# A three-matmul float32 trunk: the token forms of the output products change sides in SBUF, and the weights get a fourth place

## The chip, the cores and the metric

The kernel runs on one core of one Trainium2 chip, as one launch. The metric is the device time of that launch in microseconds (us), from the first to the last instruction and what lies around them; less is better. The core has five engines that run side by side, each through a list of instructions of its own, in order: PE (TensorE, matrix products; PEld in the profile is its weight load), DVE (VectorE), ACT (ScalarE), POOL (GpSimd) and SP (which here only issues transfers). SBUF is the on-chip memory: 128 partitions, and in each of them a run of bytes; "low" and "high" mean the byte address in a partition. PSUM is where PE puts its sums. A wait between engines is a semaphore.

## The reference, cut to what matters

A decoder trunk over 1024 tokens of width 1024, in float32: a mixing layer with a gated linear recurrence (HGRN2) and a stick-breaking attention, a channel MLP, a gMLP layer, a second channel MLP, a last norm.

```python
for layer in range(2):
    h = rms_norm(x, mix_norm[layer])
    if layer == 0:
        proj = h @ ab_w_in[0]                    # 1024 x 3584
        ...                                      # recurrence and attention
        mix = concat([oa, ob]) @ ab_w_out[0]     # 1024 x 1024
    else:
        gated = chunked_gmlp(h @ gm_w_in[0], ln_g, ln_b, gm_ws, gm_bs)   # 1024 x 6144
        mix = gated @ gm_w_out[0]                # 3072 x 1024
    x = x + mix
    h = rms_norm(x, mlp_norm[layer])
    x = x + square(relu(h @ mlp_w1[layer])) @ mlp_w2[layer]    # 1024 x 4096, 4096 x 1024
return rms_norm(x, final_norm)
```

## The kernel before, in words

**Every product is three matmuls.** A float32 operand is split into `hi`, its value rounded to the matmul's float32r (an ACT copy, L190 or L738), and `lo`, the rest (a DVE subtract, L191 or L739). `mm3` (L181 to L183) then adds hi by hi, hi by lo and lo by hi into one PSUM tile. A matmul has a stationary operand of 128 x 128, loaded by PEld, and a moving one of 128 x 512; the profile writes `acc<-f1h,whi` for a moving `f1h` over a stationary `whi`.

**The big matrix products go by seven instead of eight.** From about 640 us on each weight matrix is cut in blocks of 2 x 2, and a block's product is made of seven products P1 to P7 of sums of sub-blocks (*forms*), on the weights' side and on the tokens' side. There are three pairs of stages: *inward* (`inward`: `w1`, `gm_in`, `w1` of the second MLP) with 8, 6 and 8 blocks, and *outward* (`outward`: `w2`, `gm_out`, `w2`) with 4, 3 and 4. Before the second pair `gmlp` makes the half of `gm_in` that is normed; there the tokens are the stationary operand.

- In *inward* the seven token forms are made once for a stage (`form0` and `half1_forms`, L836 to L866) and stay; the weights are loaded (`raw`), added to forms on DVE (L888 to L896) and split into `whi` and `wlo`. One product is 24 matmuls, in the order P1, P2, P6, P7, P5, P4, P3. Results go through `x` tiles and are stored to `f_d` as the next stage's token forms by POOL (L939).
- In *outward* a product is 48 matmuls: both its token forms come from `f_d` into the tiles `fb` and are split into `f1h` and `f1l`, which then move over the weights, one half of them in `raw`, `whi`, `wlo`, the other in `fr`, `fh`, `fl`. Results are added to the `x` tiles (L1065).

**Tags.** All these tiles are 4096 bytes in a partition and belong to a tag with a number of places. A tile's split may only start when the place that it gets has been left by its last reader. Before the change: `raw` 6 places, `whi` and `wlo` 3 each (`U_W`), `fh` and `fl` 3 each, `fr` 6, `fb` 4, `f1h` and `f1l` 6 each. The inward token forms share these tags (`new_form`, L779): P1, P2, P7 lie in `f1h`/`f1l`, P6 in `fb`, P5 and one half of P4 in `fr`, the rest in `fh`/`fl`.

**Where they lie.** A pool on the left side grows from low addresses, one on the right from the top. In the built program before, `raw`, `whi`, `wlo`, `nx`, `fh`, `fl`, `fb` and `fr` fill the bytes from 20,256 to 143,136 (the DMA scratch of 16,384 bytes and constants lie below), `f1h` lies at 147,424 to 172,000, `f1l` at 172,000 to 196,576, and the eight `x` tiles above.

**What sets the order.** The kernel gives its operations in program order; the layer that records them lays out each engine's list by its own reckoning of when operands and places are there, so that a change of places changes lists too. Weight splits keep their order among themselves on ACT, loads on SP. At the start of an inward stage the steps `lead` (`Entry.lead`: sums of squares, norm, `forms1`) run while P1 and P2 of the first two blocks are on PE: the second half of the tokens is scaled (L772, eight operations), and the forms P7, P6, P5, P4, P3 are made (L852 to L863 with their splits) before PE can go on to P6 of block 0.

Of the kernel before, what the change touches and what calls it, by code (L numbers as in the profile page):

```python
# [6 lines left out]
F32 = mybir.dt.float32  # L7
# [7 lines left out]
P = 128  # L15
# [10 lines left out]
RAW_SLOTS = 5  # L26
U_RAW, U_W = 6, 3

# [4 lines left out]
class Pair:  # L33
    def __init__(self, hi, lo):
        self.hi, self.lo = hi, lo
# [62 lines left out]
class Tags:  # L98


    def __init__(self, tc, bufs):
        self.bufs = bufs
        self.pool = tc.alloc_tile_pool(name="u", bufs=1, side="left", reuse_waits="tile")
        self.release = self.pool.release
# [5 lines left out]
def trunk(tc, x_in, mix_norm, mlp_norm, w1, w2, ab_in, ab_out, lb_logits, hgrn_norm,  # L110
# [4 lines left out]
    with ctx:  # L115
# [597 lines left out]
        def u_tile(tag, dt=F32):  # L713

            pool = main["f1"] if tag in ("f1h", "f1l") else main["u"]
            return pool.tile([P, 2, H], dt, tag=tag, name=tag)

        def u_pair(h, l):
            return Pair(u_tile(h, F32R), u_tile(l, F32R))
# [59 lines left out]
        def new_form(f, k2):  # L779
            if f in (P1, P2, P7):  # L780
                t = u_pair("f1h", "f1l")
            elif f == P6:
                t = u_pair("fb", "fb")
            elif f == P5:
                t = u_pair("fr", "fr")
            elif f == P4:
                t = u_pair("fr", "fr") if k2 == 0 else u_pair("fh", "fl")
            else:
                t = u_pair("fh", "fl")
            form[f, k2] = t  # L790
            return t

        def make_form(f, k2, src):
            t = new_form(f, k2)
            split(t.hi, t.lo, src)
# [45 lines left out]
        def half1_forms(gcol, rb):  # L841
# [6 lines left out]

            sums = [u_tile("fh") for k2 in range(2)]
            b11, b21, b12, b22 = xp[0][0:2], xp[0][2:4], xp[1][0:2], xp[1][2:4]  # L850
            for k2 in range(2):
                vec.tensor_tensor(out=sums[k2], in0=b22[k2], in1=b12[k2], op=ALU.subtract)  # L852
                make_form(P7, k2, sums[k2])
            make_form(P3, 0, b22[0])
            for k2 in range(2):
# [6 lines left out]
            for k2 in range(2):  # L862
                vec.scalar_tensor_tensor(out=sums[k2], in0=sums[k2], scalar=-1.0, in1=b21[k2],  # L863
                                         op0=ALU.mult, op1=ALU.subtract)
                make_form(P4, k2, sums[k2])
            make_form(P3, 1, b22[1])  # L866

# [244 lines left out]
        def first_half0():  # L1112
            main["f1"] = tc.alloc_tile_pool(name="f1", bufs=6, side="right", reuse_waits="tile")
            e = main["e"] = Entry(G_MLP, "rm")

            def big():
                return rawp.tile([P, 2, H], F32, tag="raw", name="raw")

            e.squares(0, range(4), big)
            e.norm0(po_ps)  # L1120
            e.form0(P1)
            e.form0(P2)

        def main_open():
            pools["act"].release()
            rawp.release()
            wpool.release()
            pools["ps"].release()
            main["u"] = Tags(tc, {"raw": U_RAW, "nx": 2, "whi": U_W, "wlo": U_W, "fh": 3, "fl": 3, "fr": 6,
                                  "fb": 4, "wg": 2, "cc": 2})  # L1130
            main["mps"] = tc.alloc_tile_pool(name="mps", bufs=4, space=PSUM, reuse_waits="tile")
# [182 lines left out]
        def gate_operands(b, i, j):  # L1314
# [8 lines left out]
            if (b, i) not in gm:  # L1323
                cb = 4 * b + 2 * i
                wg = main["u"].tile([P, 2, P], F32, tag="wg", name="wg")
                cc = main["u"].tile([P, 2, P], F32, tag="cc", name="cc")
                load(flat(cc), cc_d[cb // 8][:, (cb % 8) * P:(cb % 8 + 2) * P])
                for s in range(2):
                    g = (cb + s) // 3
                    load(wg[:, s, :], wt_d[:, g * P:(g + 1) * P])  # L1330
                gm[b, i] = wg, cc
# [51 lines left out]
        main["mps"].release()  # L1383
        main["f1"].release()
        main["u"].release()
# [38 lines left out]
```

## Time and profile before

| | us |
|---|---|
| median of 3 runs (lowest, highest) | 2743.43 (2742.97, 2746.48) |
| the profiled execution's own time | 2744.25 |
| its span, first to last instruction | 2742.3 |
| PE busy (12489 matmuls) | 2640.1, 96% |
| DVE busy | 1820.9, 66% |
| ACT busy | 1019.4, 37% |
| mean granted TensorE clock | 0.988 |

The busy time of PE counts matmuls that overlap as pipelined, so 96% does not say that PE could not be faster; how long one matmul keeps the next from starting is read from the start times in the timeline. An idle time in square brackets is that of the engine just before an instruction, and after the arrow stands what ended it.

### The profile page before, as it was taken

To read this page: it belongs to the slowest core of one execution; us is meant where nothing else is said; L and a number is where in the kernel's file an instruction comes from. 1 tells how busy PE (TensorE), PEld (TensorE's weight loads), DVE (VectorE), ACT (ScalarE), POOL (GpSimd) and SP (SyncE) were. 2 spreads that over 40 slices of the span, in tenths; PEclk is the share of its full clock that TensorE was granted. 3 is DMA by queue.
4 is the path that set the end of the run, shared out by engine and by line. 5 is a ranking of instruction groups with operands and counts; after the bars stand their busy time and mean duration, and the time that the engine had idled before them with its cause. 6 is when DMAs were issued, how large, how long until landed. Compare 5 with 4: busy or idle time off the path is not lost.

```text
span 2742.3 us, 31530 instructions
## 1 busy us (share of the span) xinstructions
PE 2640.1 (96%) x12489; PEld 2143.1 (78%) x12489; DVE 1820.9 (66%) x2046; ACT 1019.4 (37%) x1281; POOL 152.5 (6%) x261
## 2 busy tenths in 40 slices
PE   8999999997999999999899999999997999999998
PEld 7888867685888878887688887877876888878887
DVE  4545464756766687777855666677778666687774
ACT  4212144543333343343433454443334333343343
POOL 1000000000101100000000100000000111000000
PEclk9999999998999999999999999999998999999999
DMA  4111111332545383444233454565431544483341
GB/s 153 43 32 47 43 35 58 108 108 68 184 140 183 124 301 131 159 162 145 73 119 114 138 194 161 191 255 199 169 131 59 167 151 141 160 305 117 131 159 62
DMA packets 204826, 371.62 MB, mean 136 GB/s; under 512 B 12072, under 2 KB 120328, under 8 KB 204680
## 3 DMA queue, kind: packets, MB, share of 16 engines
q1 hardware_dynamic: 173896, 257.93, 28.5%
q0 software_dynamic: 30784, 111.69, 10.5%
q8 instruction: 98, 1.61, 0.2%
q14 instruction: 48, 0.39, 0.0%
HBM read 253.71 MB, written 115.87 MB: 135 GB/s over the span
## 4 chain that ended last, share of the span: by engine, by line
PE 83%; DVE 9%; issue 3%; DMA 3%; ACT 2%; POOL 0%; SPq 0%; DVEq 0%; ACTq 0%; POOLq 0%
PE acc L182 21%; PE acc L183 21%; PE acc L181 21%; PE mm L181 4%; PE mm L183 4%; PE mm L182 4%; PE sm L393 1%; DVE e L551 1%; PE acc L1354 1%; DVE sig L555 1%; DVE x L772 1%; DMA nx<-v_d 1%; PE po L181 1%; DMA fr<-in_gm_w_out 1%; ACT whi L738 0%
## 5 line engine op out<-in xcount | busy, mean ns | idle before, releaser
L738 ACT ACTIVATE whi<-raw 128x1024 fp32r<-128x1024 f32 x273 | 288.6, 1058 | 956.9 <-PE acc L182 754.0
L739 DVE TENSOR_TENSOR wlo<-raw,whi 128x1024 fp32r<-128x1024 f32 x273 | 333.3, 1221 | 392.8 <-ACT whi L738 389.4
L181 PE MATMUL acc<-f1h,whi 128*128 128x512 f32 x1144 | 454.6, 398 | 11.9 <-ACT f1h L738 8.0
L182 PE MATMUL acc<-f1l,whi 128*128 128x512 f32 x1144 | 454.5, 397 | 2.0 <-DVE f1l L739 1.8
L183 PE MATMUL acc<-f1h,wlo 128*128 128x512 f32 x1144 | 453.7, 397 | 0.4 <-DVE wlo L739 0.4
L181 PEld LDWEIGHTS acc<-f1h,whi 128*128 128x128 f32 x1144 | 214.9, 188 | 67.0 <-ACT f1h L738 10.6
L182 PEld LDWEIGHTS acc<-f1l,whi 128*128 128x128 f32 x1144 | 215.3, 188 | 57.2 <-DVE f1l L739 4.0
L183 PEld LDWEIGHTS acc<-f1h,wlo 128*128 128x128 f32 x1144 | 215.3, 188 | 53.8 <-DVE wlo L739 1.1
L182 PE MATMUL acc<-f1l,fh 128*128 128x512 f32 x616 | 243.7, 396 | 0.0
L181 PE MATMUL acc<-f1h,fh 128*128 128x512 f32 x616 | 243.5, 395 | 0.0
L183 PE MATMUL acc<-f1h,fl 128*128 128x512 f32 x616 | 243.4, 395 | 0.0
L1065 DVE TENSOR_TENSOR x<-x,acc 128x1024 f32<-128x1024 f32 x154 | 187.1, 1215 | 34.9 <-PE acc L183 27.0
L181 PE MATMUL mm<-ah,whi 128*128 128x512 f32 x448 | 181.6, 405 | 0.0
L739 DVE TENSOR_TENSOR f1l<-fb,f1h 128x1024 fp32r<-128x1024 f32 x154 | 181.2, 1217 | 0.2 <-ACT f1h L738 0.2
L183 PE MATMUL mm<-ah,wlo 128*128 128x512 f32 x448 | 179.5, 401 | 0.0
L182 PE MATMUL mm<-al,whi 128*128 128x512 f32 x448 | 178.7, 399 | 0.0
L738 ACT ACTIVATE f1h<-fb 128x1024 fp32r<-128x1024 f32 x154 | 152.0, 1044 | 12.2 <-DMA fb<-f_d 12.2
L181 PEld LDWEIGHTS acc<-f1h,fh 128*128 128x128 f32 x616 | 116.0, 188 | 28.5
L182 PEld LDWEIGHTS acc<-f1l,fh 128*128 128x128 f32 x616 | 115.7, 188 | 28.5
L183 PEld LDWEIGHTS acc<-f1h,fl 128*128 128x128 f32 x616 | 115.7, 188 | 28.2
L939 POOL DMA_DIRECT2D f_d<-x x150 | 80.1, 534 | 751.6 <-DVE x L1007 351.9
L65 DVE TENSOR_TENSOR wlo<-raw,whi 128x1024 fp32r<-128x1024 f32 x44 | 53.8, 1222 | 100.8 <-ACT whi L64 80.7
(281 smaller groups left out, 4903.3 us busy)
## 6 DMA issues: line engine op xcount, KB each, us to landing
fb<-f_d SPq DMA_DIRECT2D x154, 512.0 KB, 4.8
f_d<-x POOLq DMA_DIRECT2D x150, 512.0 KB, 3.3
raw<-in_mlp_w SPq DMA_DIRECT2D x96, 512.0 KB, 4.6
raw<-in_gm_w_in SPq DMA_DIRECT2D x54, 512.0 KB, 4.6
fr<-in_mlp_w SPq DMA_DIRECT2D x32, 512.0 KB, 10.1
raw<-in_ab_w_in SPq DMA_DIRECT2D x28, 512.0 KB, 4.4
x_d<-x POOLq DMA_DIRECT2D x24, 512.0 KB, 2.9
x<-x_d SPq DMA_DIRECT2D x24, 512.0 KB, 7.4
```

Source lines behind the costliest of these rows:

```text
L65: nc.vector.tensor_tensor(out=lo, in0=raw, in1=hi.bitcast(F32), op=ALU.subtract)
L181: pe.matmul(out=ps, lhsT=a[0], rhs=b[0], start=start, stop=False, skip_group_check=s)
L182: pe.matmul(out=ps, lhsT=a[0], rhs=b[1], start=False, stop=False, skip_group_check=s)
L183: last_mm[0] = pe.matmul(out=ps, lhsT=a[1], rhs=b[0], start=False, stop=stop, skip_group_check=s)
L393: mm = pe.matmul(out=p3[:, c, :].rearrange("p (b m) -> p b m", m=m), lhsT=kr[:, c * P:(c + 1) * P], rhs=qv[:, c, :, 1, :], start=True, sto ...
L551: vec.tensor_tensor_scan(out=e[:, 0:w][:, ::-1], data0=keep[:, 0:w][:, ::-1], data1=d1[:, ::-1], initial=init, op0=ALU.mult, op1=ALU.max)
L555: vec.tensor_tensor(out=sig[:, 0:w], in0=sig[:, 0:w], in1=e[:, 1:w + 1], op=ALU.mult)
L738: in_turn("hi", lambda: act.activation(t.hi, raw, AF.Copy))
L739: vec.tensor_tensor(out=t.lo, in0=raw, in1=t.hi.bitcast(F32), op=ALU.subtract)
L772: vec.scalar_tensor_tensor(out=xt[half][k], in0=xt[half][k], scalar=gn[:, gcol + k:gcol + k + 1], in1=rb, op0=ALU.mult, op1=ALU.mult)
L939: nc.gpsimd.dma_start(out=f_d[f][b], in_=flat(t))
L1065: last_add[0] = vec.tensor_tensor(out=t, in0=t, in1=ps, op=op)
```

## The change

`new_form` and the pools change. On the left side now lie `raw`, `whi` and `wlo`, `nx`, `f1h`, `fh`, `fl`, `f1l`; on the right `fb`, `fr`, `wg`, `cc`. `whi` and `wlo` get a fourth place each; the DMA scratch is cut from 16,384 to 8,192 bytes, and the two extra tiles take that room. Inward, P1 now lies in `fb`, P2 and one half of P7 in `fr`, P6 and the other half of P7 in `fh`/`fl`, and P5, P4, P3 in `f1h`/`f1l`, whose places the next outward stage uses. The sums from which the forms are made take two places of `f1h` instead of `fh`, and P3's first half is no longer made between P7 and P6.

In the built program after, `f1h` lies at 77,600 to 102,176, `fh` and `fl` at 102,176 to 126,752, `f1l` at 126,752 to 151,328, `fb` at 151,520 to 167,904 and `fr` from there to 192,480. The operations of each engine are the same in number; their order moves.

```diff
--- before.py
+++ after.py
@@ -24,7 +24,8 @@
 EPS = 1e-6
 W_SLOTS = 4
 RAW_SLOTS = 5
-U_RAW, U_W = 6, 3
+U_RAW, U_W = 6, 4
+SCRATCH = 8192
 
 G_MIX, G_MLP, G_FIN, G_HN, G_LB, G_LG, G_LBI = 0, 16, 32, 40, 44, 48, 72
 LEVELS = (1, 2, 4, 8, 16, 32, 64)
@@ -98,9 +99,9 @@
 class Tags:
 
 
-    def __init__(self, tc, bufs):
+    def __init__(self, tc, side, bufs):
         self.bufs = bufs
-        self.pool = tc.alloc_tile_pool(name="u", bufs=1, side="left", reuse_waits="tile")
+        self.pool = tc.alloc_tile_pool(name="u" + side, bufs=1, side=side, reuse_waits="tile")
         self.release = self.pool.release
 
     def tile(self, shape, dt, tag, name):
@@ -712,7 +713,7 @@
 
         def u_tile(tag, dt=F32):
 
-            pool = main["f1"] if tag in ("f1h", "f1l") else main["u"]
+            pool = main["r"] if tag in ("fb", "fr") else main["u"]
             return pool.tile([P, 2, H], dt, tag=tag, name=tag)
 
         def u_pair(h, l):
@@ -777,16 +778,14 @@
             nc.gpsimd.dma_start(out=x_d[half * 4 + m2], in_=flat(xp[half][m2]))
 
         def new_form(f, k2):
-            if f in (P1, P2, P7):
+            if f == P1:
+                t = u_pair("fb", "fb")
+            elif f == P2 or (f, k2) == (P7, 0):
+                t = u_pair("fr", "fr")
+            elif f in (P6, P7):
+                t = u_pair("fh", "fl")
+            else:
                 t = u_pair("f1h", "f1l")
-            elif f == P6:
-                t = u_pair("fb", "fb")
-            elif f == P5:
-                t = u_pair("fr", "fr")
-            elif f == P4:
-                t = u_pair("fr", "fr") if k2 == 0 else u_pair("fh", "fl")
-            else:
-                t = u_pair("fh", "fl")
             form[f, k2] = t
             return t
 
@@ -846,12 +845,11 @@
                     for j in range(2):
                         scaled(1, 2 * (k0 + k2) + j, gcol, rb)
 
-            sums = [u_tile("fh") for k2 in range(2)]
+            sums = [u_tile("f1h") for k2 in range(2)]
             b11, b21, b12, b22 = xp[0][0:2], xp[0][2:4], xp[1][0:2], xp[1][2:4]
             for k2 in range(2):
                 vec.tensor_tensor(out=sums[k2], in0=b22[k2], in1=b12[k2], op=ALU.subtract)
                 make_form(P7, k2, sums[k2])
-            make_form(P3, 0, b22[0])
             for k2 in range(2):
                 vec.scalar_tensor_tensor(out=sums[k2], in0=sums[k2], scalar=-1.0, in1=b11[k2],
                                          op0=ALU.mult, op1=ALU.subtract)
@@ -863,7 +861,8 @@
                 vec.scalar_tensor_tensor(out=sums[k2], in0=sums[k2], scalar=-1.0, in1=b21[k2],
                                          op0=ALU.mult, op1=ALU.subtract)
                 make_form(P4, k2, sums[k2])
-            make_form(P3, 1, b22[1])
+            for k2 in range(2):
+                make_form(P3, k2, b22[k2])
 
         def one_bank():
             return pair_ps()[:, 0, :]
@@ -1110,7 +1109,7 @@
 
 
         def first_half0():
-            main["f1"] = tc.alloc_tile_pool(name="f1", bufs=6, side="right", reuse_waits="tile")
+            main["r"] = Tags(tc, "right", {"fb": 4, "fr": 6, "wg": 2, "cc": 2})
             e = main["e"] = Entry(G_MLP, "rm")
 
             def big():
@@ -1126,8 +1125,8 @@
             rawp.release()
             wpool.release()
             pools["ps"].release()
-            main["u"] = Tags(tc, {"raw": U_RAW, "nx": 2, "whi": U_W, "wlo": U_W, "fh": 3, "fl": 3, "fr": 6,
-                                  "fb": 4, "wg": 2, "cc": 2})
+            main["u"] = Tags(tc, "left", {"whi": U_W, "wlo": U_W, "f1h": 6, "f1l": 6, "fh": 3,
+                                          "fl": 3, "raw": U_RAW, "nx": 2})
             main["mps"] = tc.alloc_tile_pool(name="mps", bufs=4, space=PSUM, reuse_waits="tile")
 
         def main_run(_):
@@ -1322,8 +1321,8 @@
                                scale=gm["rs"][:, tb:tb + 1], bias=gm["nm"][:, tb:tb + 1])
             if (b, i) not in gm:
                 cb = 4 * b + 2 * i
-                wg = main["u"].tile([P, 2, P], F32, tag="wg", name="wg")
-                cc = main["u"].tile([P, 2, P], F32, tag="cc", name="cc")
+                wg = main["r"].tile([P, 2, P], F32, tag="wg", name="wg")
+                cc = main["r"].tile([P, 2, P], F32, tag="cc", name="cc")
                 load(flat(cc), cc_d[cb // 8][:, (cb % 8) * P:(cb % 8 + 2) * P])
                 for s in range(2):
                     g = (cb + s) // 3
@@ -1381,7 +1380,7 @@
 
         stream.run()
         main["mps"].release()
-        main["f1"].release()
+        main["r"].release()
         main["u"].release()
         at["xb"].release()
         at["xa"].release()
@@ -1408,7 +1407,8 @@
     import concourse.bacc as bacc
     from concourse.bass_utils import run_bass_kernel_spmd
 
-    nc = bacc.Bacc("TRN2", target_bir_lowering=False, num_devices=1)
+    nc = bacc.Bacc("TRN2", target_bir_lowering=False, num_devices=1,
+                   dynamic_dma_scratch_size=SCRATCH)
     arrays, args = {}, []
     named = [(n, np.ascontiguousarray(inputs[n])) for n in _INS]
     named.append(("c_f32", _constants()))
```

**Place one: ACT, start of the first inward stage.** These are the rows before; `whi_5745` is the weight split of block 0's P7, `whi_5750` that of its P6, `nx_5592<-acc_5678` the spread norm, the two copies from `acc` the results of P1, and L190 the forms' splits.

```order
L944 ACTIVATE nx_5591<-acc_5754 128x1024
L944 ACTIVATE nx_5592<-acc_5606 128x1024
L190 ACTIVATE fh_5706<-x_4963 128x1024
L190 ACTIVATE f1h_5697<-fh_5694 128x1024
L190 ACTIVATE f1h_5702<-fh_5695 128x1024
L190 ACTIVATE fb_5711<-fh_5694 128x1024
L190 ACTIVATE fb_5716<-fh_5695 128x1024
L190 ACTIVATE fr_5721<-x_4961 128x1024
L190 ACTIVATE fr_5726<-x_4962 128x1024
L190 ACTIVATE fr_5731<-fh_5694 128x1024
L190 ACTIVATE fh_5736<-fh_5695 128x1024
L738 ACTIVATE whi_5750<-raw_5575 128x1024
```

Before the change ACT comes to `whi_5750` only when it has done the form splits. After it, ACT has at the same place:

```order
L739 ACTIVATE whi_5745<-raw_5575 128x1024
L739 ACTIVATE whi_5750<-raw_5575 128x1024
L768 ACTIVATE nx_5592<-acc_5678 128x512
L739 ACTIVATE whi_5812<-raw_5585 128x1024
L943 ACTIVATE nx_5591<-acc_5754 128x1024
L943 ACTIVATE nx_5592<-acc_5606 128x1024
L191 ACTIVATE fr_5697<-f1h_5694 128x1024
L191 ACTIVATE fh_5702<-f1h_5695 128x1024
L191 ACTIVATE f1h_5717<-x_4961 128x1024
L191 ACTIVATE fh_5707<-f1h_5694 128x1024
L191 ACTIVATE fh_5712<-f1h_5695 128x1024
L191 ACTIVATE f1h_5722<-x_4962 128x1024
```

P6's weight split moves from behind all the form splits to ahead of the spread norm, and P4's (`whi_5812`) with it.

**Place two: ACT, a little later.** `x_5845` takes P6's result of block 0, `x_5872` that of its P7, `whi_5817` is the weight split of its P5. Before:

```order
L738 ACTIVATE whi_5812<-raw_5585 128x1024
L190 ACTIVATE fh_5740<-x_4964 128x1024
L944 ACTIVATE x_5845<-acc_5606 128x1024
L738 ACTIVATE whi_5817<-raw_5585 128x1024
L738 ACTIVATE whi_5875<-raw_5575 128x1024
L944 ACTIVATE x_5872<-acc_5847 128x1024
```

Here P5's weight split follows at once on the copy of P6's result. After the change ACT has there:

```order
L943 ACTIVATE x_5845<-acc_5606 128x1024
L191 ACTIVATE f1h_5736<-x_4963 128x1024
L191 ACTIVATE f1h_5740<-x_4964 128x1024
L943 ACTIVATE x_5872<-acc_5847 128x1024
L739 ACTIVATE whi_5817<-raw_5585 128x1024
L739 ACTIVATE whi_5875<-raw_5575 128x1024
```

P5's weight split now stands behind the copy of P7's result.

**Place three: DVE, start of the first outward stage.** L1065 (after: L1064) adds a result to an `x` tile that was loaded again from `x_d`; L891 (after: L890) makes the weight forms of P6, whose splits are `wlo_7763` and `fl_7768`; `f1l_7772` is P6's first token split. Before:

```order
L739 TENSOR_TENSOR f1l_7686<-fb_7679,f1h_7685 128x1024
L1065 TENSOR_TENSOR x_7693<-x_7693,acc_7699 128x1024
L739 TENSOR_TENSOR wlo_7753<-raw_7595,whi_7752 128x1024
L1065 TENSOR_TENSOR x_7694<-x_7694,acc_7725 128x1024
L739 TENSOR_TENSOR fl_7758<-fr_7601,fh_7757 128x1024
L891 TENSOR_TENSOR raw_7595<-raw_7595,raw_7661 128x1024
L891 TENSOR_TENSOR fr_7601<-fr_7601,fr_7671 128x1024
L1065 TENSOR_TENSOR x_7693<-x_7693,acc_7785 128x1024
L739 TENSOR_TENSOR wlo_7763<-raw_7595,whi_7762 128x1024
L739 TENSOR_TENSOR fl_7768<-fr_7601,fh_7767 128x1024
L739 TENSOR_TENSOR f1l_7772<-fb_7689,f1h_7771 128x1024
```

Here the first two additions stand ahead of both forms. After the change DVE has there:

```order
L740 TENSOR_TENSOR fl_7758<-fr_7601,fh_7757 128x1024
L961 TENSOR_TENSOR x_7646<-x_7534,x_7643 128x1024
L890 TENSOR_TENSOR raw_7595<-raw_7595,raw_7661 128x1024
L963 SCALAR_TENSOR_TENSOR x_7647<-x_7646,x_7444 128x1024
L966 TENSOR_TENSOR x_7643<-x_7444,x_7643 128x1024
L968 SCALAR_TENSOR_TENSOR x_7648<-x_7647,x_7507 128x1024
L740 TENSOR_TENSOR wlo_7763<-raw_7595,whi_7762 128x1024
L890 TENSOR_TENSOR fr_7601<-fr_7601,fr_7671 128x1024
L1064 TENSOR_TENSOR x_7693<-x_7693,acc_7699 128x1024
L740 TENSOR_TENSOR fl_7768<-fr_7601,fh_7767 128x1024
L1064 TENSOR_TENSOR x_7694<-x_7694,acc_7725 128x1024
L740 TENSOR_TENSOR f1l_7772<-fb_7689,f1h_7771 128x1024
```

The weight forms of P6 move ahead of the first addition to an `x` tile.

## Rows read from the trace of the kernel before

**Rows 1.** Waits of PE: engine, line, waited for: us in total, times, longest
```profile
PE acc L181 <- ACT whi L738: 35.6, 3, 15.9
...
PE acc L182 <- DVE wlo L739: 9.9, 2, 9.0
PE acc L181 <- ACT f1h L738: 8.0, 6, 2.4
```

**Rows 2.** Groups of PE instructions by form: busy us, mean ns of one, idle before
```profile
L181 PE MATMUL acc<-f1h,fh 128*128 128x512 f32 x616 | 243.5, 395 | 0.0
...
L182 PE MATMUL acc<-fl,whi 128*128 128x512 f32 x264 | 102.8, 389 | 0.0
```

**Rows 3.** Timeline of PE, first inward stage: start us, us, engine line op, tiles
```profile
688.04 0.39 PE L181 MATMUL acc<-f1h,whi 128*128 128x512 f32 x1
...
692.94 0.39 PE L181 MATMUL acc<-fr,whi 128*128 128x512 f32 x1
...
709.28 0.39 PE L181 MATMUL acc<-fb,whi 128*128 128x512 f32 x1
```

**Rows 4.** Timeline of PE, inside the first outward stage
```profile
1100.02 0.39 PE L181 MATMUL acc<-f1h,whi 128*128 128x512 f32 x1
...
1111.22 0.39 PE L181 MATMUL acc<-f1h,whi 128*128 128x512 f32 x1
```

**Rows 5.** Stretches: PE, PEld, DVE, ACT, POOL busy, clock, DMA share, GB/s
```profile
1020.00:1240.00 220.00, 220.00 (x944) 176.33 (x943) 163.59 (x143) 82.33 (x82) 1.07 (x2) 1.00 0.46 159
...
680.00:685.00 5.00, 5.00 (x14) 3.69 (x13) 5.00 (x6) 1.36 (x2) 0.58 (x1) 0.57 0.12 48
```

**Rows 6.** Timeline of ACT, DVE and PE, start of the first inward stage
```profile
651.35 1.06 ACT L738 ACTIVATE whi<-raw 128x1024 fp32r<-128x1024 f32 x1 [5.93 <-PE acc L182]
...
653.58 5.38 DVE L772 SCALAR_TENSOR_TENSOR x<-x,gn,nx 128x512 f32<-128x512 f32 x8
...
658.88 2.36 DVE L852 TENSOR_TENSOR fh<-x 128x1024 f32<-128x1024 f32 x2
...
661.15 1.22 DVE L191 TENSOR_TENSOR fl<-x,fh 128x1024 fp32r<-128x1024 f32 x1
...
663.16 0.40 PE L183 MATMUL acc<-f1h,wlo 128*128 128x512 f32 x1
...
678.18 1.22 DVE L1006 TENSOR_TENSOR nx<-nx,acc 128x1024 f32<-128x1024 f32 x1
...
679.41 0.80 PE L181 MATMUL acc<-fb,whi 128*128 128x512 f32 x1 [15.86 <-ACT whi L738]
```

**Rows 7.** Timeline of PE, start of the third inward stage
```profile
2109.82 0.79 PE L181 MATMUL acc<-fb,whi 128*128 128x512 f32 x1 [15.80 <-ACT whi L738]
```

**Rows 8.** Timeline of DVE and PE, start of the first outward stage
```profile
986.56 1.22 DVE L1065 TENSOR_TENSOR x<-x,acc 128x1024 f32<-128x1024 f32 x1 [3.70 <-DMA x<-x_d]
...
991.31 1.22 DVE L891 TENSOR_TENSOR raw<-raw 128x1024 f32<-128x1024 f32 x1
...
995.81 0.73 PE L181 MATMUL acc<-f1h,whi 128*128 128x512 f32 x2 [2.38 <-ACT f1h L738]
997.71 0.49 PE L181 MATMUL acc<-f1h,whi 128*128 128x512 f32 x1 [1.16 <-ACT f1h L738]
```

**Rows 9.** Timeline of PE, start of the third outward stage
```profile
2422.55 0.74 PE L181 MATMUL acc<-f1h,whi 128*128 128x512 f32 x2 [1.22 <-ACT f1h L738]
2424.44 0.50 PE L181 MATMUL acc<-f1h,whi 128*128 128x512 f32 x1 [1.16 <-ACT f1h L738]
```

**Rows 10.** Timeline of PE, `gmlp` before the second pair of stages
```profile
1334.39 0.80 PE L182 MATMUL acc<-wlo,f1h 128*128 128x512 f32 x1 [8.97 <-DVE wlo L739]
...
1343.56 0.50 PE L182 MATMUL acc<-wlo,fb 128*128 128x512 f32 x1 [0.97 <-DVE wlo L739]
```

**Rows 11.** Transfers by line: KB each, median us from issue to landing; POOL's own time
```profile
f_d<-x POOLq DMA_DIRECT2D x150, 512.0 KB, 3.3
...
980.88 0.53 POOL L939 DMA_DIRECT2D f_d<-x  x1 [0.60 <-DVE x L969]
```

## The prediction

> **What bounds the kernel now.** I read the waits of PE first, then the groups of its matmuls by operands, then the timeline where the waits lie. PE is busy nearly all the time, so time can come from two places: the few stretches in which it waits, and the rate of the stream itself.
>
> The waits are few. 35.6 us are three waits for a `whi`, 9.9 two waits for a `wlo`, 8.0 six waits for an `f1h` [rows 1]. Two of the three are 15.86 and 15.80 us long and stand at the same place, P6 of block 0 in the first and third inward stages [rows 6, 7].
>
> The rate has two levels, and the reader should see them side by side. Matmuls that move `f1h` over `fh` last 395 ns, those that move `fl` over `whi` 389, with no idle time ahead of either [rows 2]. What counts is the distance between starts. From 688.04 to 692.94 us 21 matmuls of P7 start (moving operand in `f1h`, `f1l`): 4.90/21 = 233.3 ns each. From 692.94 to 709.28 follow the 72 of P5, P4 and P3, moving from `fr`, `fh`, `fl`: 16.34/72 = 226.9 ns [rows 3]. It is the same stage, the same kind of weights and the same width, and neither set of forms is being written any more. In the outward stage, where all moving operands lie in `f1h` and `f1l`, 48 matmuls take 11.20 us: 233.3 ns again [rows 4]. The clock was granted in full there (1.00 in the stretch from 1020 to 1240 us) [rows 5]. What the slow ones share is the address: in the built program `f1h` and `f1l` begin at byte 147,424, all the fast ones end by 143,136. I read the 6.4 ns as the price of a moving operand that lies high.
>
> The Trainium skill, "TensorE: Matmul & The Clock Gate", section "Back-to-back issue gap", gives the distance between matmuls as a function of the columns and the clock alone, about 216 ns for 512 columns; no address enters. Neither level in the trace is 216, and there are two of them at one width and one clock, so the trace departs from it; by that rule the term for the placement would be nothing (first rival).
>
> **Term 1, the placement.** Outward there are 11 blocks x 7 products x 48 = 3696 matmuls, all slow now. Inward there are 22 x 7 x 24 = 3696, of which P1, P2, P7 are slow, 3/7 or 1584. After the change P1, P2 and half of P7 still move from the high side (`fb`, `fr`): 2.5/7, or 1320. The rest moves from the low side, except that `f1l` runs up to byte 151,328: from its highest place (147,232 on) 296 matmuls move, from the one below it (143,136 to 147,232), where the trace has nothing, another 296. So 5280 slow matmuls become 1616 to 1912, and 3368 to 3664 get 6.4 ns shorter: 21.6 to 23.4 us. I take 22.5. The ends for the range are 0, if the address is not the cause, and 23.4. Nothing else should hold the stream at the old rate: from 1020 to 1240 us DVE is busy for 163.59 of 220 us, and a weight load takes 176.33/943 = 187 ns, well under 226.9 [rows 5]. If that cover were gone, the term would shrink by as much.
>
> **Term 2, the start of the first and third inward stages.** Before, P6's `whi` stands on ACT behind the form splits, and on DVE its form is added (L891) behind sixteen operations on the forms. PE's last matmul before it starts at 663.16 us, P6 begins at 679.41 [rows 6], P5 at 692.94 [rows 3]. With four places the `whi` of P6 takes the one that P2 of block 0 leaves; that is the event which releases P7's `whi` at 651.35 now [rows 6]. So its split is done before the eight scalings begin at 653.58, and these begin no later. What is late next is the list of DVE. The scalings end and the first form begins at 658.88; from there two operations take until 661.15, 1.135 us each [rows 6]. By the new order P6's two `lo` splits are the ninth and tenth operations. The tenth ends at 658.88 + 10 x 1.135 = 670.2, the ninth 1.1 earlier; PE can start P6 in earnest at 669.2 and finishes it at 669.2 + 24 x 0.227 = 674.7. P7 then needs the PSUM tile that P2's result of block 0 leaves, when DVE has added it (L1005, now at 678.18 as L1006 [rows 6]). In the new list that is the seventeenth operation: 658.88 + 17 x 1.135 = 678.2. So P7 runs from 678.3 to 683.9. P5's weight form comes seven operations after that add, done at 678.2 + 7 x 1.135 = 686.1; its `whi`, on ACT behind the copy of P7's result, takes 1.06 (the length of an ACT split [rows 6]) until 687.3, its `wlo` until 688.5. The third matmul of P5 needs the `wlo`, so P5 begins in effect at 688.1 instead of 692.94: 4.8 less. It is far from 15.9, because two other waits take its place (P7 for the PSUM tile, P5 for its weights).
>
> The waits also cost clock: from 680 to 685 us, after the long idle time, 0.57 was granted [rows 5], so part of it ran at 1.2 GHz. That is 5 x 0.43 = 2.2 us. If the shorter idle times cost as much, P6 ends at 676.9, still before the PSUM tile comes free, and nothing is added. Bounds for one such place: 0, if P5's weights come later still, and 692.94 - 663.4 - 48 x 0.227 = 18.6, if PE never waits. I take 4.8, twice: 9.6. Both places have the same lists after the change.
>
> **Term 3, the start of the outward stages.** DVE stands 3.70 us waiting for an `x` tile from DRAM at 986.56, with P6's weight forms (L891 at 991.31) behind it; PE then waits 2.38 and 1.16 us for P6's token splits, which follow on ACT [rows 8]. In the new list the weight forms are ahead of that wait, and five operations behind it P6's second token split is done: 986.56 + 5 x 1.135 + 0.1 = 992.3. PE came to the wait at 995.81 - 2.38 = 993.4 and will come 96 x 6.4 ns = 0.6 sooner, at 992.8. So both waits go: 3.5 us. The third stage has the same new order: 1.22 + 1.16 = 2.4 [rows 9]. The second keeps its list, and PE only comes to the same waits 0.6 us sooner, so 0.6 of term 1 is lost there. Net 5.3; bounds 0 and 8.0 (all six waits of [rows 1]).
>
> **Term 4, `gmlp`.** PE waits 8.97 us for a `wlo` of P7 that stands on DVE behind sixteen operations on the forms [rows 10]. In the new list there are again sixteen between the scalings and it, so this wait stays, though a fourth place is there. The 0.97 after it (P6's `wlo`) goes, since that split now stands ahead of the forms on ACT. 1.0; bounds 0 and 9.9.
>
> **The sum.** 22.5 + 9.6 + 5.3 + 1.0 = 38.4. The profiled execution took 2744.25, 0.8 above the median of the runs, 2743.43. 2744.25 - 38.4 = 2705.9, and 2705 in terms of the median. The first 630 us (recurrence, attention) keep their work; their tiles only move down by 8 KB, for which I put nothing.
>
> **Rivals.**
> - *Placement does nothing.* The 6.4 ns come from something else that `f1h` has, and move with the tag. For it: in the trace tag and address cannot be told apart. Against it: inward, `f1h` and `fr` are used in the same way, and differ in address alone. Terms 2 to 4 without the 0.6 remain, 16.5: 2743.4 - 16.5 = 2727. The rule on the gap cited above says the same of the placement. Chance 0.12.
> - *Placement alone.* The moved lists give back elsewhere what they gain, as P5's late weights already do with two thirds of the long wait: 2743.4 - 22.5 = 2721. Chance 0.08.
> - *The long waits go wholly*, since PE's own progress lets DVE's list run earlier than I reckon: 2 x 18.6 for term 2, all 8.0 and 9.9 for the others less 0.6: 22.5 + 37.2 + 7.4 + 9.9 = 77 at the most. Halfway between that and my sum lies 2685. Against it: every step of term 2 after 658.88 hangs on DVE alone, which is busy without a break. Chance 0.05.
> - *Slower: the halved DMA scratch holds up POOL's stores.* Now a store takes 0.53 us on POOL and 3.3 to land [rows 11], and the next is issued while it is under way. A block inward takes 7 x 24 x 0.227 = 38.1 us and writes seven `x` tiles of the eight, so its seven result tiles come free in time as long as one store, taken alone, costs less than 38.1/7 = 5.4 us; from about 5.4 + 38.4/(22 x 7) = 5.7 us the whole change is a loss. At 6 us: 22 x (42 - 38.1) = 86 us more, 2791. Against it: even one at a time a store now costs 0.53 + 3.3 = 3.8 us. The Trainium skill, "SBUF — State Buffer", section "SBUF size: 192, 224, or 256?", calls this scratch the ring of descriptors of the POOL queue; no run here shows how full it gets. Chance 0.04.
>
> **How the numbers follow.** The forecast has 0.71; its own range, with 21.6 to 23.4 for term 1, 3 to 9 us for each place of term 2, and 0 to 10 for the rest together, is 2692 to 2713. To hold 8 in 10 with the unknown costs I reach to the first two rivals: 2689 to 2725. Faster or slower by over 0.2%, 5.5 us, is about what a measurement of this kernel can tell from no change. All cases but the last lie beyond it on the faster side, 0.96; since lists also moved where I did not follow them, I give 0.93 to faster, 0.03 to the same, 0.04 to slower.
>
> **What would show it.** In the changed profile: outward stretches with 48 matmuls in 10.9 us, and `f1h` over `fh` at 389 ns (term 1); P6 of block 0 beginning ten us after P2 of block 1 or less, with two shorter waits behind it, for a DVE add and a `whi` (term 2); no wait for `f1h` at the first and third outward starts, and one at the second (term 3); the wait of 9 us in `gmlp` still there (term 4). Wrong it would be if the outward matmuls still start 233 ns apart, if POOL waits for room before its transfers, or if new waits for `whi` show up inside the stages.

## The result and the profile after

The changed kernel takes 2700.4 us (median of four runs, 2697.6 to 2703.5), the kernel before, run beside it, 2744.95. The ratio is 0.984, with a 95% interval from 0.982 to 0.985. 2705 was forecast, with a range from 2689 to 2725. The profiled execution took 2697.58 us for 2744.25 before, its span is 2695.8 us, its mean granted clock 0.992.

**The waits.** The view of PE's waits answers to [rows 1].

```profile
PE acc L183 <- DVE wlo L740: 8.5, 1, 8.5
...
PE acc L1353 <- DVE acc L1356: 7.4, 11, 1.4
PE acc L182 <- ACT fh L191: 6.7, 2, 3.4
PE acc L182 <- ACT whi L739: 5.6, 3, 4.0
...
PE acc L182 <- DVE nx L1005: 3.2, 2, 1.9
...
PE acc L182 <- ACT f1h L739: 1.7, 2, 1.2
```

Of 35.6 us for a `whi` 5.6 are left (the longest, 4.0, lies ahead of the first inward start and was there before), of six waits for an `f1h` two. In their place stand short waits for a form (`fh`) and for a PSUM tile (`nx`), all at the starts of the first and third inward stages. The wait for a `wlo` in `gmlp` stays.

**The rate.** One line of the groups of matmuls; it answers to the first row of [rows 2].

```profile
L182 PE MATMUL acc<-f1h,fh 128*128 128x512 f32 x616 | 239.9, 389 | 0.0
```

Next the timeline of PE in the first inward stage, then two rows from the first outward stage, 48 matmuls apart; they answer to [rows 3, 4].

```profile
714.86 0.39 PE L182 MATMUL acc<-f1h,whi 128*128 128x512 f32 x1
...
731.19 0.39 PE L182 MATMUL acc<-fb,whi 128*128 128x512 f32 x1
...
736.79 0.39 PE L182 MATMUL acc<-fr,whi 128*128 128x512 f32 x1
...
742.39 0.39 PE L182 MATMUL acc<-fh,whi 128*128 128x512 f32 x1
...
1084.70 0.39 PE L182 MATMUL acc<-f1h,whi 128*128 128x512 f32 x1
...
1095.58 0.39 PE L182 MATMUL acc<-f1h,whi 128*128 128x512 f32 x1
```

From 714.86 to 731.19 72 matmuls move `f1h` and `f1l`: 226.8 ns each. The 24 of `fb` behind them take 5.60 us, 233.3 ns each, and the 24 of `fr` the same. The two levels have changed places with the tags. Outward, 48 matmuls now take 10.88 us, 226.7 ns each. All this is as forecast. But `f1l` is fast up to its highest place, which ends at byte 151,328, while before `f1h` was slow from byte 147,424 on. Height can't explain that, and the experiments begin there.

**The start of the first inward stage.** Timeline of PE and of ACT's weight splits, and two stretches (columns as in [rows 5]); they answer to [rows 6].

```profile
644.48 2.01 ACT L739 ACTIVATE whi<-raw 128x1024 fp32r<-128x1024 f32 x2 [0.38 <-DMA raw<-in_mlp_w]
651.53 1.06 ACT L739 ACTIVATE whi<-raw 128x1024 fp32r<-128x1024 f32 x1 [5.04 <-PE acc L183]
...
667.11 0.65 PE L182 MATMUL acc<-fh,whi 128*128 128x512 f32 x1 [3.38 <-ACT fh L191]
669.43 0.79 PE L183 MATMUL acc<-fl,whi 128*128 128x512 f32 x1 [1.67 <-DVE fl L192]
678.51 0.50 PE L182 MATMUL acc<-fr,whi 128*128 128x512 f32 x1 [1.37 <-DVE nx L1005]
685.45 0.50 PE L182 MATMUL acc<-f1h,whi 128*128 128x512 f32 x1 [1.11 <-ACT x L943]
698.30 0.47 PE L182 MATMUL acc<-f1h,whi 128*128 128x512 f32 x1 [1.30 <-ACT whi L739]
703.86 0.39 PE L182 MATMUL acc<-fh,whi 128*128 128x512 f32 x1
```

```profile
665.00:670.00 5.00, 1.22 (x2) 0.69 (x3) 5.00 (x5) 2.12 (x2) 0.00 (x0) 0.73 0.00 0
670.00:675.00 5.00, 5.00 (x15) 3.93 (x14) 5.00 (x6) 3.16 (x3) 0.00 (x0) 0.59 0.02 3
```

P6 starts at 667.11 instead of 679.41 and waits only for its token form. Then P7 waits for its PSUM tile (678.51). P4, P5 and P3 are done at 703.86; before, the same 72 matmuls were done at 709.28 [rows 3]. So 5.4 us are left of the 12.3 by which P6 came earlier.

**The start of the first outward stage.** The first fence is the kernel before (two rows of PE, then two stretches), the second the same two matmuls after.

```profile
991.87 0.39 PE L181 MATMUL acc<-f1h,fh 128*128 128x512 f32 x1
...
1003.42 0.39 PE L182 MATMUL acc<-f1l,whi 128*128 128x512 f32 x1
...
995.00:1000.00 5.00, 2.97 (x7) 1.94 (x8) 5.00 (x5) 5.00 (x6) 0.00 (x0) 0.83 0.14 34
1000.00:1005.00 5.00, 5.00 (x19) 3.95 (x19) 3.87 (x4) 0.49 (x1) 0.00 (x0) 0.83 0.89 287
```

```profile
985.42 0.39 PE L182 MATMUL acc<-f1h,fh 128*128 128x512 f32 x1
...
990.86 0.39 PE L182 MATMUL acc<-f1h,fh 128*128 128x512 f32 x1
```

By count of matmuls these are places 3834 and 3858 of the three-matmul stream in both kernels. They lie 11.55 us apart before and 5.44 after. Of the 6.1 us, 3.5 are the two waits of [rows 8], 0.2 the distance of 24 matmuls, and by an estimate from the two stretches 1.7 the clock: 0.83 was granted in them, 10 x 0.17. The other 0.7 is not traced to a cause. After, no wait is left there.

**Where the time came from**, by the start of the same matmul (counted along the stream) before and after: first inward start 5.7 us, third 5.3; starts of the first and third outward stages 7.3 and 6.0, of which 1.3 each is distance; the rest of the three outward stages with the lead into `gmlp` 6.8 + 5.7 + 7.8 = 20.3; `gmlp` 1.55; the rest of the first and third inward stages 1.15; the second inward stage -1.3; ahead of the stages -0.3. That is 45.7 at the last matmul; the spans differ by 46.5.

### The profile page after: what moved, and what is told of

Same layout as the page of the kernel before. It is cut to its first block, busy times and chain, and to the rows that moved or that the text cites. A ratio compares the mean times of both kernels' runs of the same rounds, so it can differ in the third digit from the quotient of the medians.

```text
span 2695.8 us, 31404 instructions
## 1 busy us (share of the span) xinstructions
PE 2614.2 (97%) x12489; PEld 2144.2 (80%) x12489; DVE 1819.3 (67%) x2046; ACT 1016.0 (38%) x1281; POOL 153.5 (6%) x261
## 4 chain that ended last, share of the span: by engine, by line
PE 83%; DVE 8%; DMA 3%; issue 2%; ACT 2%; POOL 0%; SPq 0%; ACTq 0%; DVEq 0%; POOLq 0%
PE acc L183 21%; PE acc L184 21%; PE acc L182 21%; PE mm L182 4%; PE mm L184 4%; PE mm L183 4%; PE sm L394 1%; DVE e L552 1%; PE acc L1353 1%; DMA nx<-v_d 1%; DVE sig L556 1%; ACT whi L739 1%; DVE x L773 1%; PE po L182 1%; DVE wlo L740 0%
## 5 line engine op out<-in xcount | busy, mean ns | idle before, releaser
L740 DVE TENSOR_TENSOR wlo<-raw,whi 128x1024 fp32r<-128x1024 f32 x273 | 333.2, 1222 | 228.5 <-ACT whi L739 225.6
L182 PE MATMUL acc<-f1h,whi 128*128 128x512 f32 x1144 | 448.1, 392 | 5.7 <-ACT x L943 2.2
L183 PE MATMUL acc<-f1l,whi 128*128 128x512 f32 x1144 | 446.4, 390 | 3.1 <-DVE f1l L740 3.1
L184 PE MATMUL acc<-f1h,wlo 128*128 128x512 f32 x1144 | 445.2, 389 | 0.0
L1064 DVE TENSOR_TENSOR x<-x,acc 128x1024 f32<-128x1024 f32 x154 | 187.6, 1218 | 160.0 <-PE acc L184 156.1
L739 ACT ACTIVATE fh<-fr 128x1024 fp32r<-128x1024 f32 x77 | 81.8, 1062 | 404.3 <-PE acc L183 301.8
```

Source lines behind the costliest of these rows:

```text
L182: pe.matmul(out=ps, lhsT=a[0], rhs=b[0], start=start, stop=False, skip_group_check=s)
L183: pe.matmul(out=ps, lhsT=a[0], rhs=b[1], start=False, stop=False, skip_group_check=s)
L184: last_mm[0] = pe.matmul(out=ps, lhsT=a[1], rhs=b[0], start=False, stop=stop, skip_group_check=s)
L739: in_turn("hi", lambda: act.activation(t.hi, raw, AF.Copy))
L740: vec.tensor_tensor(out=t.lo, in0=raw, in1=t.hi.bitcast(F32), op=ALU.subtract)
L1064: last_add[0] = vec.tensor_tensor(out=t, in0=t, in1=ps, op=op)
```

## The experiments

All are timed beside the kernel before. The offset of a tile is its byte address in the built program modulo 256. Left-side tiles have 32 and right-side tiles 224 in both kernels, unless unused space is put in; the pads are

```
const.tile([P, N // 4], F32, name="pad_left")      # moves every tile on the left up by N bytes
pad = ctx.enter_context(tc.tile_pool(name="pad", bufs=1, side="right"))
pad.tile([P, N // 4], F32, name="pad_right")       # moves every tile on the right down by N bytes
```

**Is it the height?** Kernel before, right pad of 64.

> The kernel before, with 64 bytes per partition of unused space put at the base of the right side, so that f1h and f1l begin 64 bytes lower (147,360 for 147,424) and nothing else differs. Theory of the height (the prediction's): f1h still lies high, its matmuls stay at 233.3 ns, time as before within 2 us. Theory of the offset: 147,424 lies 96 bytes past a multiple of 128, 147,360 lies 32 past one, as all the fast operands do; all 5280 matmuls that move f1h or f1l then go at 226.9 ns, 5280 x 6.4 = 34 us less, of which some 2 are lost again in waits at the outward starts: ratio about 0.988, and matmuls of f1h over fh at 389 ns. Theory of the side or the tag: as the height.

2744.4 us, ratio 0.9998 (0.9988 to 1.0007): nothing. The group of `f1h` over `fh`:

```profile
L183 PE MATMUL acc<-f1h,fh 128*128 128x512 f32 x616 | 244.6, 397 | 0.0
```

It is as slow as before. The theory of the offset in this form (96 past a multiple of 128 slow, 32 fast) falls. Kernel after, right pad of 64:

> The kernel after, with the same 64 bytes of unused space at the base of the right side: fb and fr now lie 32 bytes past a multiple of 128 instead of 96. Theory of the offset: the 1320 inward matmuls that move from fb and fr go at 226.9 instead of 233.3 ns, 1320 x 6.4 = 8.4 us less than the kernel after, about 2692 us, ratio to the kernel before about 0.981. Theory of the height (with a bound above 151,328, the end of f1l, which is fast there): fb and fr stay at 233.3 ns, about 2700 us.

2699.3 us, ratio 0.983 (0.982 to 0.985), the same as the change; the 24 matmuls of `fb` again take 5.59 us, 233 ns each:

```profile
731.97 0.40 PE L184 MATMUL acc<-fb,whi 128*128 128x512 f32 x1
...
737.56 0.40 PE L184 MATMUL acc<-fr,whi 128*128 128x512 f32 x1
```

Kernel after, 96 bytes on both sides, so that every form lies at 128:

> The kernel after, with 96 bytes of unused space at the base of the right side and 96 on the left, so that every form begins at a multiple of 128. Theory of the offset in steps of 64 (a run of 128 bytes that begins in the first half costs 226.9, in the second 233.3): all matmuls at 226.9 ns, about 2692 us. Theory of an offset that counts byte by byte (6.4 ns for 64 bytes, so 3.2 less from 32 to 0): 223.7 ns for all 7392, 6072 x 3.2 + 1320 x 9.6 = 32 us less than the kernel after, about 2668 us. Theory of the height or the side: about 2700 us, with fb and fr at 233.3 ns.

2693.3 us, ratio 0.981 (0.980 to 0.982), where the steps of 64 had 2692. `fb` is fast, 5.44/24 = 226.7 ns, on the right side and at the same height but for 96 bytes:

```profile
732.22 0.39 PE L185 MATMUL acc<-fb,whi 128*128 128x512 f32 x1
...
737.66 0.39 PE L185 MATMUL acc<-fr,whi 128*128 128x512 f32 x1
```

Height and side fall with that. Steps of 64 don't stand either: the two runs before it put the slow operands at 160, in the same half of a run of 128 bytes as 32, and they stayed slow. What the three runs share is another thing: the fast matmuls have their moving operand and their weights at one offset, the slow ones at two. The next runs were made for this.

**Is it the equal offset of the two operands?** Kernel after, left pad of 192. `fb` and `fr` don't move; the weights under them do.

> The kernel after, with 192 bytes of unused space on the left, so that every tile on the left moves up by 192 bytes and fb and fr on the right don't move at all. All forms and weights are then 224 bytes past a multiple of 256; in the kernel before, that is where the slow f1h lay and the fast operands lay at 32. Theory that the two operands of a matmul have to lie at the same offset: fb and fr over weights of the left go from 233.3 to 226.9 ns without having moved, nothing gets slower, 1320 x 6.4 = 8.4 us less than the kernel after, about 2692 us. Theory that some offsets of the moving operand are slow by themselves (96, 160, 224 past a multiple of 256): all 6072 matmuls that move from the left go to 233.3 ns, 6072 x 6.4 = 39 us more, about 2739. Theory of the height or the side: about 2700.

2694.3 us, ratio 0.981 (0.980 to 0.982). `fb` has not moved by a byte and is fast, 5.43/24 = 226.3 ns:

```profile
732.36 0.39 PE L183 MATMUL acc<-fb,whi 128*128 128x512 f32 x1
...
737.79 0.39 PE L183 MATMUL acc<-fr,whi 128*128 128x512 f32 x1
```

All else now moves from offset 224, where `f1h` was slow before, and is fast. No property of the moving operand alone can do that. Kernel after, right pad of 96, so that only `fb` and `fr` lie at 128:

> The kernel after, with 96 bytes of unused space at the base of the right side: fb and fr lie at a multiple of 128 (128 past one of 256), where all forms were fast together in the run with 96 bytes on both sides; the weights on the left stay 32 past a multiple of 256. Theory of the same offset for both operands: fb and fr over these weights stay at about 233 ns, 2700 us. Theory that a multiple of 128 is a fast place for a moving operand by itself: fb and fr at 226.9 ns, 2692 us.

2702.6 us in one run, and 5.62/24 = 234 ns, though 128 was a fast place when all lay there:

```profile
730.83 0.40 PE L184 MATMUL acc<-fb,whi 128*128 128x512 f32 x1
...
736.45 0.39 PE L184 MATMUL acc<-fr,whi 128*128 128x512 f32 x1
```

Kernel after, right pad of 160, a difference of 32 bytes:

> The kernel after with 160 bytes at the base of the right side: fb and fr lie 32 bytes off the offset of the weights, nearer than in any run so far (64, 96, 128 and 192 off were all slow). If only an equal offset is fast, 232 to 234 ns for fb and fr and about 2700 us; if what counts is the block of 64 bytes, they share none (32 and 64 past a multiple of 256), and the same; if a small offset costs in proportion, some 228 to 230 ns.

2701.9 us in one run, 5.60/24 = 233.3 ns: a small difference costs as much as a large one.

```profile
731.32 0.40 PE L184 MATMUL acc<-fb,whi 128*128 128x512 f32 x1
...
736.92 0.39 PE L184 MATMUL acc<-fr,whi 128*128 128x512 f32 x1
```

**What is the placement worth without moving a tag?** Kernel before, right pad of 192.

> The kernel before, with 192 bytes of unused space at the base of the right side: f1h and f1l begin at 147,232, which is 32 past a multiple of 256 as the weights and the other forms on the left are; no tag is moved and no order changed. Theory of the same offset: all 5280 matmuls that move f1h or f1l at 226.9 ns, 5280 x 6.4 = 34 us less, some 2 of it lost at the outward starts, so 2712 and a ratio of about 0.988; the waits of the first and third inward starts still 15.8 us. Theory of the height, now with a threshold between 147,232 and 151,520, or of the side or the tag: 2744, f1h at 233.3 ns.

2717.3 us, ratio 0.990 (0.989 to 0.9915): 27.6 us less, for 192 unused bytes.

```profile
L183 PE MATMUL acc<-f1h,fh 128*128 128x512 f32 x616 | 239.9, 389 | 0.0
```

All 5280 matmuls are fast; 5280 x 6.6 = 34.8, and 7 of that don't show. 5 of them are longer waits of PE for splits, which it reaches sooner (for `whi` 36.2 us instead of 35.6, for `f1h` 8.6 instead of 8.0, for `wlo` 13.9 instead of 10.9, for `f1l` 2.9 instead of 1.8); the other 2 are not traced. The size was over-estimated, the mechanism holds. Kernel before with the halved scratch and a right pad of 448, which puts `f1h` 256 bytes off the weights modulo 512:

```
dynamic_dma_scratch_size=8192     # and a right pad of 448
```

> The kernel before with the halved scratch alone and 448 bytes at the base of the right side: f1h and f1l then lie 256 bytes off the offset of the weights modulo 512 (at 32, the weights at 288). Two questions at once, told apart by the distances. If offsets count modulo 256, f1h goes at 226.9 ns and the time is that of the run with 192 bytes, 2717; if modulo 512, 233.3 ns and 2745. If the halved scratch costs or gives something by itself, the time stands apart from both.

2719.4 us, ratio 0.991 (0.989 to 0.992): offsets count modulo 256, and the halved scratch alone shows no effect beyond the intervals.

```profile
L183 PE MATMUL acc<-f1h,fh 128*128 128x512 f32 x616 | 240.7, 391 | 0.0
```

**What are the fourth place and the new order worth?** Kernel before with the fourth place:

```
U_RAW, U_W = 6, 4                 # and dynamic_dma_scratch_size=8192
```

> The kernel before with the fourth weight place and the halved DMA scratch of the kernel after, but with every tag where it was. It tells the terms of the fourth place from that of the addresses. Theory that the lead waits hang on the weight place: the wait of P6 at the first and third inward starts shrinks, the distances stay at 226.9 and 233.3 ns, and the time falls by 5 to 10 us, to about 2735. Theory that the lead gained only because the forms run in another order: no change, 2743. Theory that the halved scratch costs something: over 2744.

2735.1 us, ratio 0.996 (0.995 to 0.998): some 10 us. P6 starts ten us sooner, as in the changed kernel, and waits for its form alone. The waits for `f1h` at the outward starts are all there (the last row is from the waits of PE).

```profile
669.16 0.79 PE L181 MATMUL acc<-fb,whi 128*128 128x512 f32 x1 [4.51 <-ACT fb L190]
...
PE acc L181 <- ACT f1h L738: 7.9, 6, 2.0
```

The kernel after with three places:

```
U_RAW, U_W = 6, 3
```

> The kernel after with three weight places instead of four; tags, sides and the halved scratch stay. The distances are those of the kernel after. Theory that the term of the lead hangs on the fourth place: P6's weights are late again at the first and third inward starts, with waits of 10 us or more for a whi, and the time is 8 to 12 us above the kernel after, about 2710. Theory that the new order of the forms alone made it: about 2700.

2720.8 us, ratio 0.991 (0.990 to 0.993), 20 above the changed kernel and not 8 to 12. The long waits are back, whole, with one of 1.1 us behind each:

```profile
679.79 0.80 PE L182 MATMUL acc<-fh,whi 128*128 128x512 f32 x1 [15.86 <-ACT whi L739]
682.11 0.79 PE L184 MATMUL acc<-fh,wlo 128*128 128x512 f32 x1 [1.09 <-DVE wlo L740]
```

By the starts of matmuls this kernel loses 2.3 and 1.5 us against the kernel before at the two inward starts, and 2.8 in `gmlp`. So there the new tags and order cost time as long as the place is missing. Another 2.8 are lost just ahead of the third inward start, where PE waits no longer than in the changed kernel but is granted less clock, 0.64 in the stretch below (columns as in [rows 5]) and 1.00 in the changed kernel at that place. Why is open; the kernel with 96 bytes on both sides loses as much there, with four places.

```profile
2035.00:2040.00 5.00, 4.41 (x12) 2.50 (x12) 2.01 (x4) 0.66 (x2) 1.61 (x2) 0.64 0.08 30
```

At the first and third outward starts this kernel has no wait for an `f1h`: that part comes from the new tags and order, which no run separates, and not from the place.

The kernel before with the fourth place and equal offsets, but the old tags:

```
U_RAW, U_W = 6, 4                 # scratch 8192, and a right pad of 192
```

> The kernel before with two things that were each run alone: the fourth weight place (with the halved scratch), which took 9.9 us off, and 192 bytes at the base of the right side, which took 27.6 off. No tag is moved and the order of the forms stays. If the two gains add, 2745 - 37.5 = 2707 us; what the kernel after with equal offsets (2694) has beyond that is then the worth of the new tags and order themselves, 13 us, mostly at the starts of the outward stages. If a faster stream only runs into the weights and forms sooner, less than the sum, about 2712.

2706.2 us, ratio 0.986 (0.984 to 0.987): 38.7 us, within the intervals the sum of the two gains. The waits at the first outward start are still there:

```profile
987.96 0.73 PE L183 MATMUL acc<-f1h,whi 128*128 128x512 f32 x2 [2.92 <-ACT f1h L740]
989.86 0.79 PE L183 MATMUL acc<-f1h,whi 128*128 128x512 f32 x1 [1.16 <-ACT f1h L740]
```

With all distances equal, the changed tags and order are worth 2706.2 - 2694.3 = 12 us. The kernels after with equal offsets (2693 and 2694) are the fastest here, 6 to 7 us below the change.

## Why the prediction was right, and where not

- **Term 1, the placement: the size nearly right by luck, the mechanism wrong.** The step "I read the 6.4 ns as the price of a moving operand that lies high" failed. The price is that of two operands at different offsets modulo 256. The change helped because it put most moving forms on the side of the weights, and with them on their offset; where a pad gives equality (192 bytes on the left or the right, 96 on both), sides don't matter. In the inward and outward products the trace of before could not show it, since side, height, tag and offset went together there, and I took the first that fitted. `gmlp` held a sign: there `whi` and `wlo`, which lie low, move over `f1h` and `f1l` at 229 ns instead of 227 (rows in the last section), which no height of the moving operand explains. The error in size follows from it: I left `f1l`'s highest place slow and half of the next one, while 1320 matmuls are slow instead of 1616 to 1912. 3960 x 6.5 = 25.7 became free, above my upper end of 23.4; about 24 show in the stretches above (20.3 + 2 x 1.3 + 1.15).
- **The rule of the gap.** The Trainium skill, "TensorE: Matmul & The Clock Gate", section "Back-to-back issue gap", has no address in it. It gives about 216 ns for 512 columns as the gap of a matmul taken alone, and about 131 ns for a stream of weight loads and matmuls; the prediction named only the first. The runs agree with neither figure, nor with my height: at one width and one clock 226.7 and 233 ns both occur, and 192 unused bytes turn one into the other. The rival that said the same of the placement (2727) is out.
- **Term 2, the inward starts: right, but for the last step.** 4.8 each were forecast, 5.7 and 5.3 came. P6 in earnest at 669.2 (669.43), P7 at 678.3 (678.51), P5, P4, P3 done at 688.1 + 16.3 = 704.4 (703.86). P6's `whi` is split ahead of the scalings, as said, at 651.53. The step that failed is P5's late weights: in the built program PE starts P4 ahead of P5, which covers them. In their place P4 waits 1.1 us for the copy of P7's result, and P3 for its `whi`, 1.3 us (0.4 in the third stage). The clock fell to 0.73 and 0.59 behind the shorter idle times, and cost nothing more, since P7 has to wait for DVE anyway. That the place makes this term is shown from both sides (some 10 us with it alone, the waits whole without it).
- **Term 3, the outward starts: right in kind, half its size.** 3.5 + 2.4 - 0.6 = 5.3 were forecast, 6.0 + 4.6 and nothing lost at the second are 10.6. Both waits went at the first and third; the step that failed is that I priced idle time alone and left out the clock behind it, though term 2 had reckoned with just that: 0.83 was granted for ten us here and 0.66 for five at the third stage, an estimated 1.7 us each. 0.6 more is what the second stage did not lose; the last 1.3 is not traced. That the new tags and order make it, and not the place, is shown: no such wait without the fourth place in the changed kernel, all of them with it in the old order.
- **Term 4, `gmlp`: right.** The wait for a `wlo` stays, 8.5 for 8.97; the second one goes. 1.55 for 1.0.
- **What I had no term for:** the second inward stage loses 1.3 us. Its waits for an `acc` (L1353 in the view of PE's waits, L1354 before) are eleven of 7.4 us in all instead of six of 6.1. They come with the fourth place: all eight kernels that have it show 9 to 11 such waits, 7.4 to 11.9 us in all, the five without it five or six, 5.7 to 6.3. The first row is the kernel before with the place alone, the second the kernel after without it. Why the place brings them is not traced.

```profile
PE acc L1354 <- DVE acc L1357: 7.8, 10, 2.1
```

```profile
PE acc L1353 <- DVE acc L1356: 5.9, 5, 1.2
```

- **Placement alone (2721).** Three places gave 2720.8, but not as this rival had it. In the change the moved lists give back little of the gain elsewhere, the 1.3 above; without the place the new tags and order lose in the inward starts, in `gmlp` and to the clock about what they win at the outward starts.
- **The scratch.** One store took POOL 0.53 us as before, and lands in 3.9 us for 3.3 [rows 11]:

```profile
f_d<-x POOLq DMA_DIRECT2D x150, 512.0 KB, 3.9
```

  The longer landing goes with the fourth place, not with the scratch: both kernels with the halved scratch and three places (the padded kernel before and the kernel after) land in 3.3, the kernel before with the fourth place in 3.9. The padded kernel with the halved scratch lost about 2 us to the one without, within both intervals. The slower case is out.

The sum of 38.4 us became 45.7 at the last matmul of the two profiled executions and 44.5 between the medians. Term 3 gave 5.3 more, term 1 about 1.6, term 2 1.4, term 4 0.5; the second inward stage and the part ahead of the stages took 1.6 back.

## What to carry to other kernels

Where matmuls of one width and one clock keep two distances, list the addresses of both operands, not of one, and change a single property by some unused bytes before any tag is moved: here 192 bytes gave 27.6 of the 44.5 us. Price a wait of PE with the clock behind it, by the granted clock of the stretch that follows. A further place for a buffer and a new order of the work should be tried apart and together, since here the new tags and order gave about nothing without the place (24.1 us in all, where an estimate from the stretches gives the placement about 24) and 12 us with it.

## What the runs showed that was not expected

Where a form of 512 columns moves over weights at full granted clock, a matmul starts 226.3 to 226.8 ns after the one before it when the two operands lie at the same byte offset modulo 256 (seen at 32, 128 and 224, and 256 bytes apart modulo 512), and on average 233 to 234 ns after it when they differ, by 32, 96, 128 or 192 bytes alike.

In `gmlp`, where the weights move over the forms, the price is not always the same. The rows are 24 matmuls apart, at a granted clock of 1.00: first the kernel before (moving operand at 32, stationary at 224), then the right pad of 64 (stationary at 160), then the right pad of 192 (both at 32).

```profile
1308.53 0.39 PE L183 MATMUL acc<-whi,f1l 128*128 128x512 f32 x1
...
1314.03 0.39 PE L183 MATMUL acc<-whi,f1l 128*128 128x512 f32 x1
```

```profile
1310.89 0.39 PE L185 MATMUL acc<-whi,f1l 128*128 128x512 f32 x1
...
1316.46 0.40 PE L185 MATMUL acc<-whi,f1l 128*128 128x512 f32 x1
```

```profile
1298.45 0.39 PE L185 MATMUL acc<-whi,f1l 128*128 128x512 f32 x1
...
1303.89 0.39 PE L185 MATMUL acc<-whi,f1l 128*128 128x512 f32 x1
```

That is 229, 232 and 227 ns each. So equal offsets are the fast case here too, but 32 against 224 costs a third of what it costs the other way round. Whether the direction of the difference or the role of the operands makes that is not tested.

Whether it is a matmul's own weights that count or those being loaded for the next one is open: both lie on one side nearly always in these kernels. So is what the chip does with the two addresses.
